# Values and gate of the retention layer: four pairs of k-tiles in seven products instead of three, in five of eight groups

## The chip, the core and the metric

The kernel runs on one core of a Trainium2 chip. The metric is the device time of one execution in microseconds (us). TensorE (PE) multiplies, VectorE (DVE) and ScalarE (ACT) do elementwise work, GpSimd (POOL) takes a few roots, SyncE (SP) issues the loads. Each engine runs its own list of instructions in the order written down when the program was built; an instruction that waits holds up everything behind it on its engine.

## The reference

A two-layer decoder trunk on 256 tokens of width 2048 in float32. Layer 0 mixes tokens by retention, layer 1 by latent attention, and a SwiGLU network follows each. The change lies in one product of the retention layer:

```python
def retention(x, positions, w_in, gn_g, w_out):
    proj = x @ w_in                       # 256 x 2048 by 2048 x 12288
    q, k, v, g = jnp.split(proj, [RET_QK, 2 * RET_QK, 2 * RET_QK + RET_VD], axis=-1)
    ...                                   # 8 heads; v and g have 512 columns per head
    scores = jnp.einsum('bhqd,bhkd->bhqk', qi, ki) * decay_in
    y = jnp.einsum('bhqk,bhkv->bhqv', scores, vi) + ...
    ...                                   # y is normalized per head
    out = (jax.nn.silu(g) * y)
    return out @ w_out
```

## The kernel before

**A float32 product in three.** Every operand is split into a rounded part (hi, a cast on ACT) and the rest (lo, a subtraction on DVE); `split` issues both. A product is then hi·hi + hi·lo + lo·hi: three matmuls of 128x512. The weights come from memory in tiles of 128 rows by 1024 columns (512 KB) and are split on the way, so a plain tile costs one ACT cast and one DVE subtraction of 128x1024.

**Groups.** Values and gate are made in eight groups `vg_group(0)` to `vg_group(7)`, one per head, names `rvg0` to `rvg7`. A group multiplies all 256 tokens (two halves of 128) by 1024 weight columns: 512 of v, 512 of the gate. It sums over 16 k-tiles in four PSUM banks `(t, c)`, t the token half and c the column half. A plain k-tile takes 12 matmuls.

**Seven products.** Two neighbouring k-tiles form a pair, and token half, column half and k-tile make it a 2x2 by 2x2 block product. `first_sevens` computes its first `n` pairs with seven block products instead of eight (Winograd's form of Strassen's scheme): 21 matmuls for 24. The sums of weight blocks are made on DVE, for every pair of every group. The left sums, of the input, are made once and kept in `ins[p]`. In words, for each pair `p`: `begin` loads two raw tiles `s0` and `s1`, makes t1, t2, t3 and splits b00, t2 (tile "b", two halves of 512) and t1, t3 (tile "a", 1024); `rest` splits the raw second tile (tile "c", 1024); `fourth` adds once more and splits the result (tile "d", 512).

```python
            b, a = parts("b"), parts("a")
            nc.vector.tensor_add(out=ta[:, 0:512], in0=b00, in1=b01)      # L458
            nc.vector.tensor_add(out=t2[p], in0=ta[:, 0:512], in1=b11)    # L459
            split(*half(b, 0), b00)
            split(*half(b, 1), t2[p])
            nc.vector.tensor_add(out=ta[:, 512:1024], in0=b01, in1=b11)   # L462
            split(*a, ta)
            ...
            split(*wt["c", p], raw1[p])                                   # rest
            ...
            nc.vector.tensor_add(out=t2[p], in0=t2[p], in1=raw1[p][:, 0:512])  # L473, fourth
            split(*wt["d", p], t2[p])
```

A group of values and gate therefore runs in four stretches on PE: A, the products of `begin` for all pairs (with the nine matmuls `ry` of the head before, of `mixed`, behind the first pair); B, those of `rest`, with DVE's sums `u`, `v` and c01, c11 over the banks (L485 to L495); C, those of `fourth`; D, the plain tiles, called by their k-tile `w6` to `w15`. Eight transposes `ztp` of the head before fall somewhere between. The feed-forward layers build their groups (`gu`) by the same function with four pairs, `GU_SEVENS = 4`.

**What orders the work.** The loads are all on SP's queue, the code is written in program order, and a scheduler then fixes each engine's list. Buffers are rings: 5 pairs of hi and lo tiles (`whi`, `wlo`, `WB`), 4 raw tiles (`raw`), 4 of tag `y4` for `s1`, 2 of `tsum` for `ta`. A new tile waits until the last reader of the one before it in its buffer is done. In the retention stage there are also 8 buffers of tag `yT`, one for each head's output; those not yet needed are lent to the last weight tiles of a group by `share(slots, room)`: `both` is 2 from six free slots, 1 from three, else 0 (hi and lo of so many last tiles), and `min(2, slots - 2 * both)` raw tiles (k-tiles 12 and 13; names with `x`). `later(k, fn)` runs a function k loading steps on.

Of the kernel before, what the change touches and what calls it, by code (L numbers as in the profile page):

```python
# [8 lines left out]
F32 = mybir.dt.float32  # L9
F32R = mybir.dt.float32r  # L10
# [5 lines left out]
P = 128  # L16
SEQ = 256
D = 2048
DT = D // P
NT = SEQ // P  # L20
EPS = 1e-6
RH, RK, RV = 8, 256, 512
# [13 lines left out]
DN_SEVENS = (2, 5, 7, 10, 12, 15, 17), (2, 4, 5, 7, 10, 12, 15, 17)  # L36
RTO_SEVENS = (3, 6, 9, 12), (3, 5, 6, 9, 12)
MLO_SEVENS = (3, 5), (1, 3)
QK_SEVENS, VG_SEVENS = (0, 2, 3, 3), 3

C_INV, C_ID, C_MASK, C_TWICE = 0, NF, NF + P, NF + 3 * P
C_DEC = C_TWICE + ROPE
# [16 lines left out]
def trunk(  # L59
# [19 lines left out]
    nc = tc.nc  # L79
# [8 lines left out]
    def misc_bank(name):  # L88
        return ps.tile([P, 512], F32, tag="misc", bufs=2, name=name)
# [43 lines left out]
    def later(k, fn):  # L133
        order[0] += 1
        todo.append((steps[0] + k, order[0], fn))
# [63 lines left out]
    wp = ctx.enter_context(tc.tile_pool(name="wp", bufs=1))  # L199
    RAW, WB, MV = 4, 5, 6  # L200

    def share(slots, room):

        both = 2 if slots >= 6 else 1 if slots >= 3 else 0
        return min(2, slots - 2 * both), both, room

    def split(hi, lo, src, g=None):

        if g is None:
            nc.scalar.copy(out=hi, in_=src)  # L210
            nc.vector.tensor_sub(out=lo, in0=src, in1=hi.bitcast(F32))  # L211
        else:
            nc.scalar.activation(out=hi, in_=src, func=AF.Copy, scale=g)
            nc.vector.scalar_tensor_tensor(
                out=lo, in0=src, scalar=g, in1=hi.bitcast(F32), op0=ALU.mult, op1=ALU.subtract
            )
# [18 lines left out]
    def gain(col, kt):  # L235
        return None if col is None else gcol[:, col + kt : col + kt + 1]
# [7 lines left out]
    def left_sums(a00, a01, a10, a11, sums, hi, lo):  # L244

        nc.vector.tensor_sub(out=sums[:, 0], in0=a10, in1=a11)
        nc.vector.tensor_sub(out=sums[:, 1], in0=sums[:, 0], in1=a00)
        nc.vector.tensor_sub(out=sums[:, 2], in0=a00, in1=a10)
        nc.vector.tensor_add(out=sums[:, 3], in0=sums[:, 1], in1=a01)
        split(hi, lo, sums)  # L250
# [321 lines left out]
    def hx(k):  # L572
        if k // 4 not in hT:
            hT[k // 4] = hp.tile([P, 4, 2, NT, P], F32R, tag="h8", bufs=4, name="hT")
        return hT[k // 4]
# [5 lines left out]
    def watched(pairs):  # L581


        made, held, tiles = {}, {}, [None]

        def seen(t, k0, n, part):
            for p in range(pairs):
                if k0 <= 2 * p < k0 + n:
                    held[t, p] = part[:, 2 * p - k0], part[:, 2 * p - k0 + 1]
                    if (1 - t, p) in held:  # L590
                        f, hi, lo = tiles[0](len(made))
                        left_sums(*held[0, p], *held[1, p], f, hi, lo)
                        made[p] = hi, lo

        watch[0] = seen
        return made, tiles
# [20 lines left out]
    def rms(ssq, n, tag, name):  # L617
        s = small(1, "s1", 4, f"{name}_s")
        nc.vector.tensor_reduce(out=s, in_=ssq, axis=mybir.AxisListType.X, op=ALU.add)
        v = small(1, "v1", 4, f"{name}_v")  # L620
        nc.vector.tensor_scalar(v, s, scalar1=1.0 / n, scalar2=EPS, op0=ALU.mult, op1=ALU.add)
        return rsqrt(v, 1, tag, 4, f"{name}_r")
# [141 lines left out]
    def retention():  # L764
# [15 lines left out]
            lo = wp.tile([P, 4, P], F32R, tag="al", bufs=3, name="rxl")  # L780
            return f, hi, lo

        ins, where = watched(max(*QK_SEVENS, VG_SEVENS))
        where[0] = tiles
        load_x(0, 0)
        later(0, lambda: norm_piece(0, 0, first[0], G_MIX))
# [12 lines left out]
        def qk_group(gq, spare):  # L799
            name = f"rqk{gq}"  # L800
            if gq:
                return first_sevens(h_lhs, DT, ret_qk, gq, name, QK_SEVENS[gq], lambda p: ins[p], spare)
            return group(h_lhs, DT, tile_load(ret_qk, gq, name, 1, spare), name, lead=3)

        def vg_group(h, spare):
            return first_sevens(h_lhs, DT, ret_vg, h, f"rvg{h}", VG_SEVENS, lambda p: ins[p], spare)

        with tc.tile_pool(name="rt_s", bufs=1) as sp:
            scores = {}
# [68 lines left out]
            with tc.tile_pool(name="rt_q", bufs=1) as rp, ExitStack() as copies:  # L878
                rope_c = rp.tile([P, NT, NF_R], F32, name="rope_c")
                rope_s = rp.tile([P, NT, NF_R], F32, name="rope_s")  # L880
                spare = share(3, lambda kind, name: rp.tile([P, 1024], kind, tag="spare", bufs=3, name=name))
                for gq in range(4):
                    banks = qk_group(gq, spare)
                    if gq == 0:
                        rx = [rms(first[t], D, "rx", f"first_r{t}") for t in range(NT)]
# [9 lines left out]
                banks = vg_group(0, spare)  # L895

            with tc.tile_pool(name="rt_v", bufs=1) as rp:

                yT = {}

                def spare_y(kind, name):
                    return rp.tile([P, 1024], kind, tag="yT", bufs=RH, name=name)

                def take_y(k0, n):
                    return yT[k0 // 4][:, k0 % 4 : k0 % 4 + n]

                def mixed(h, t, pr, v, sg):
                    y = misc_bank(f"ry{h}{t}")

                    terms = [  # L910
                        (pr[a][:, (kb + t) * P : (kb + t + 1) * P], v[b][:, kb, :])
                        for kb in range(t + 1)
                        for a, b in ((0, 0), (0, 1), (1, 0))
                    ]
                    for n, (left, right) in enumerate(terms):
                        nc.tensor.matmul(y, left, right, start=n == 0, stop=n == len(terms) - 1)  # L916
                    st = rp.tile([P, 6], F32, tag="bst", bufs=4, name="bst")
                    nc.vector.bn_stats(out=st, in_=y)
                    mv = rp.tile([P, 2], F32, tag="bmv", bufs=4, name="bmv")
                    nc.vector.bn_aggr(out=mv, in_=st)  # L920
                    ve = rp.tile([P, 1], F32, tag="bve", bufs=4, name="bve")
                    nc.vector.tensor_scalar(ve, mv[:, 1:2], scalar1=EPS, scalar2=None, op0=ALU.add)
                    rs = rsqrt(ve, 1, "grs", 4, "grs")
                    z = rp.tile([P, RV], F32, tag="z", bufs=2, name="z")
                    nc.vector.scalar_tensor_tensor(
                        out=z, in0=y, scalar=mv[:, 0:1], in1=sg[:, t, :],
                        op0=ALU.subtract, op1=ALU.mult,
                    )
                    nc.vector.tensor_scalar(z, z, scalar1=rs, scalar2=None, op0=ALU.mult)

                    def transposes():
                        if t == 0:
                            yT[h] = rp.tile([P, 4, NT, P], F32, tag="yT", bufs=RH, name=f"yT{h}")
                        tp = misc_bank(f"ztp{h}{t}")
                        for j in range(4):
                            nc.tensor.transpose(
                                tp[:, j * P : (j + 1) * P], z[:, j * P : (j + 1) * P], ident
                            )
                        for j in range(4):
                            nc.scalar.activation(  # L940
                                out=yT[h][:, j, t, :], in_=tp[:, j * P : (j + 1) * P], func=AF.Copy,
                                scale=gain(G_GN, h * 4 + j),
                            )

                    later(10, transposes)

                for h in range(RH):
                    if h:
                        banks = vg_group(h, share(RH - h, spare_y))
                    vh = rp.tile([P, NT, RV], F32R, tag="vh", bufs=1, name=f"vh{h}")  # L950
                    vl = rp.tile([P, NT, RV], F32R, tag="vl", bufs=1, name=f"vl{h}")
                    ph = rp.tile([P, 3 * P], F32R, tag="ph", bufs=1, name=f"ph{h}")
                    pl = rp.tile([P, 3 * P], F32R, tag="pl", bufs=1, name=f"pl{h}")
                    split(ph, pl, scores[h])
                    sg = rp.tile([P, NT, RV], F32, tag="sg", bufs=1, name=f"sg{h}")
                    for t in range(NT):
                        split(vh[:, t, :], vl[:, t, :], banks[t][0], rx[t])
                        nc.scalar.activation(
                            out=sg[:, t, :], in_=banks[t][1], func=AF.Silu, scale=rx[t]
                        )  # L960
                    for t in range(NT):
                        later(2 + t, lambda h=h, t=t, pr=(ph, pl), v=(vh, vl), sg=sg: mixed(h, t, pr, v, sg))

                gu_next[0] = watched(GU_SEVENS)
                closing(
                    take_y, RH * 4, ret_out, g_mix_post[0], G_FFN, "rto",
                    lambda name: rp.tile([P, 1024], F32, tag="sg", bufs=1, name=name), sevens=RTO_SEVENS,
                )
# [434 lines left out]
```

## Time and profile before

| | us |
|---|---|
| median of 3 runs | 2402.5 (2402.4 to 2402.98) |
| profiled execution | 2400.07 |
| its span, first to last instruction | 2398.3 |
| busy in the span: PE / DVE / ACT / POOL | 2382.3 / 2179.7 / 1500.3 / 28.5 |
| granted PE clock | 0.999 |
| stage of the eight groups of values and gate | about 197 to 556 |
| one such group, from one head's `ry` to the next | 44.7 |
| one `gu` group of the first feed-forward layer | 41.7 |

Times inside the profile count from the start of the span. "Busy" of PE covers overlapping matmuls, so how fast PE goes is read from the distance between the starts of matmuls or of stretches, not from their durations. The chain in the page is followed back from the last instruction.

### The profile page before, as it was taken

What the parts mean: (1) busy time and instruction counts of PE and PEld (TensorE: products, weight loads), DVE (VectorE), ACT (ScalarE), POOL (GpSimd) and SP (SyncE); (2) the same over time, 40 slices, a digit from 0 to 9 for tenths busy, and PEclk for the clock granted to TensorE, in tenths of its full rate; (3) what the DMA queues carried; (4) which work ended last, traced back from release to release, by engine and by line L of the source; (5) the groups of instructions that cost most, each with busy time, mean ns of one, the idle gap of its engine ahead of it and who ended that gap; (6) DMA issues with size and microseconds to landing.
All of it is one profiled execution on the core that took longest, in us unless ns stands there. A gap on an engine that the chain in (4) does not pass through costs nothing.

```text
span 2398.3 us, 30805 instructions
## 1 busy us (share of the span) xinstructions
PE 2382.3 (99%) x10843; PEld 1971.0 (82%) x10843; DVE 2179.7 (91%) x3112; ACT 1500.3 (63%) x2126; POOL 28.5 (1%) x38
## 2 busy tenths in 40 slices
PE   9999999999999999999999999999999999999998
PEld 7888888888888888888888888887888888888887
DVE  8899888888899999999988987889999999998998
ACT  6555665665666656666666666656666665666664
POOL 0000000000000000000000000000100000000000
PEclk9999999999999999999999999999999999999999
DMA  8555465545656665656456655445666565645655
GB/s 285 187 195 191 167 212 184 170 170 192 206 194 219 207 207 199 209 179 219 161 197 210 200 196 158 129 138 171 234 205 216 177 218 184 212 167 183 221 199 168
DMA packets 129611, 463.76 MB, mean 193 GB/s; under 512 B 14640, under 2 KB 15024, under 8 KB 129456
## 3 DMA queue, kind: packets, MB, share of 16 engines
q1 hardware_dynamic: 129456, 461.80, 57.7%
q8 instruction: 85, 1.39, 0.2%
q14 instruction: 70, 0.57, 0.1%
HBM read 459.64 MB, written 2.10 MB: 193 GB/s over the span
## 4 chain that ended last, share of the span: by engine, by line
PE 94%; DVE 4%; DMA 1%; issue 1%; ACT 1%; SPq 0%; POOL 0%; DVEq 0%; POOLq 0%; ACTq 0%
PE gu_b L419 37%; PE dn_b L419 15%; PE rvg_b L419 14%; PE rqk_b L419 6%; PE rto_b L419 6%; PE q L419 3%; PE dn_m L419 3%; PE mlo_b L419 2%; PE mc_b L419 1%; PE rto_m L419 1%; PE ftp L988 1%; PE ry L916 1%; PE htp L602 0%; PE rsc L861 0%; PE asc L1240 0%
## 5 line engine op out<-in xcount | busy, mean ns | idle before, releaser
L419 PE MATMUL gu_b<-gu_w_hi,hT 128*128 128x512 f32 x1296 | 353.6, 391 | 0.1
L419 PEld LDWEIGHTS gu_b<-gu_w_hi,hT 128*128 128x128 f32 x1296 | 242.3, 188 | 50.6 <-DVE hT L211 0.9
L210 ACT CAST dn_w_hi<-dn_w_raw 128x1024 fp32r<-128x1024 f32 (+1 forms) x176 | 169.1, 978 | 78.4 <-DMA dn_w_raw<-w_down 33.7
L419 PE MATMUL gu_b<-gu_w_lo,hT 128*128 128x512 f32 x648 | 200.4, 391 | 0.0
L211 DVE TENSOR_TENSOR dn_w_lo<-dn_w_raw,dn_w_hi 128x1024 fp32r<-128x1024 f32 (+1 forms) x176 | 193.8, 1130 | 7.1 <-ACT dn_w_hi L210 6.3
L419 PE MATMUL rvg_b<-rvg_w_hi,hT 128*128 128x512 f32 x576 | 157.4, 391 | 0.0
L419 PE MATMUL dn_b<-dn_w_lo,dn_ah 128*128 128x512 f32 x494 | 156.7, 390 | 0.3 <-DVE dn_w_lo L211 0.3
L419 PE MATMUL dn_b<-dn_w_hi,dn_ah 128*128 128x512 f32 x494 | 156.7, 390 | 0.0
L419 PE MATMUL dn_b<-dn_w_hi,dn_al 128*128 128x512 f32 x494 | 156.7, 390 | 0.0
L211 DVE TENSOR_TENSOR gu_w_lo<-gu_w_raw,gu_w_hi 128x1024 fp32r<-128x1024 f32 x122 | 143.6, 1223 | 6.0 <-ACT gu_w_hi L210 6.0
L419 PEld LDWEIGHTS gu_b<-gu_w_lo,hT 128*128 128x128 f32 x648 | 121.2, 188 | 26.3 <-DVE gu_w_lo L211 1.5
L210 ACT CAST gu_w_hi<-gu_w_raw 128x1024 fp32r<-128x1024 f32 x122 | 122.5, 1049 | 29.2 <-PE gu_b L419 11.3
L419 PEld LDWEIGHTS rvg_b<-rvg_w_hi,hT 128*128 128x128 f32 x576 | 107.7, 188 | 22.0
L210 ACT CAST gu_ahi<-gu_ta 128x1024 fp32r<-128x1024 f32 x80 | 84.4, 1055 | 46.7 <-PE gu_b L419 36.0
L211 DVE TENSOR_TENSOR gu_clo<-gu_s,gu_chi 128x1024 fp32r<-128x1024 f32 x80 | 97.6, 1222 | 14.7 <-ACT gu_chi L210 13.4
L419 PEld LDWEIGHTS dn_b<-dn_w_lo,dn_ah 128*128 128x128 f32 x494 | 92.7, 188 | 19.8 <-DVE dn_w_lo L211 0.7
L419 PEld LDWEIGHTS dn_b<-dn_w_hi,dn_ah 128*128 128x128 f32 x494 | 92.8, 188 | 19.2
L419 PEld LDWEIGHTS dn_b<-dn_w_hi,dn_al 128*128 128x128 f32 x494 | 92.8, 188 | 19.2
L211 DVE TENSOR_TENSOR gu_alo<-gu_ta,gu_ahi 128x1024 fp32r<-128x1024 f32 x80 | 97.8, 1223 | 7.0 <-ACT gu_ahi L210 6.9
L210 ACT CAST gu_bhi<-gu_s 128x512 fp32r<-128x512 f32 x80 | 49.7, 622 | 81.6 <-PE gu_b L419 65.9
L419 PE MATMUL rqk_b<-rqk_w_hi,hT 128*128 128x512 f32 x352 | 99.4, 396 | 1.2 <-ACT rqk_w_hi L210 1.1
L210 ACT CAST gu_chi<-gu_s 128x1024 fp32r<-128x1024 f32 x80 | 83.8, 1051 | 13.6 <-PE gu_b L419 13.4
(535 smaller groups left out, 6284.9 us busy)
## 6 DMA issues: line engine op xcount, KB each, us to landing
dn_w_raw<-w_down SPq DMA_DIRECT2D x176, 512.0 KB, 4.5
gu_s<-w_gu SPq DMA_DIRECT2D x160, 512.0 KB, 4.6
gu_w_raw<-w_gu SPq DMA_DIRECT2D x152, 512.0 KB, 3.7
rvg_w_raw<-ret_vg SPq DMA_DIRECT2D x67, 512.0 KB, 4.4
rto_w_raw<-ret_out SPq DMA_DIRECT2D x64, 512.0 KB, 4.3
rvg_s<-ret_vg SPq DMA_DIRECT2D x48, 512.0 KB, 4.2
rqk_w_raw<-ret_qk SPq DMA_DIRECT2D x43, 512.0 KB, 4.3
gu_w_xraw<-w_gu SPq DMA_DIRECT2D x40, 512.0 KB, 5.2
```

The source lines that it names most:

```text
L210: nc.scalar.copy(out=hi, in_=src)
L211: nc.vector.tensor_sub(out=lo, in0=src, in1=hi.bitcast(F32))
L419: nc.tensor.matmul(out, e[2](), e[3](), start=bank not in begun, stop=ends[bank, added.get(bank, 0)] == n, skip_group_check=bank in added,)
L916: nc.tensor.matmul(y, left, right, start=n == 0, stop=n == len(terms) - 1)
L988: nc.tensor.transpose(tp[:, b * P : (b + 1) * P], a[:, b * P : (b + 1) * P], ident)
```

## The change

Groups 2 to 6 of values and gate take four pairs by seven products; groups 0, 1 and 7 stay at three. The left sums of the fourth pair (k-tiles 6 and 7) are made by a new function `fourth_sums`, which a `later(9, ...)` puts into group 1: it adds the hi and lo parts of both k-tiles of the input together again, makes the four sums, splits them and keeps both parts in one `yT` buffer. That buffer is missing from the slots that groups 2 to 6 may lend out, so `share` gets one less there: group 2 lends one hi and lo pair instead of two, group 4 one raw tile instead of two, group 5 no hi and lo pair and two raw tiles instead of one each, group 6 one raw tile instead of two; group 3 lends as before.

```diff
-QK_SEVENS, VG_SEVENS = (0, 2, 3, 3), 3
+QK_SEVENS, VG_SEVENS = (0, 2, 3, 3), (3, 3, 4, 4, 4, 4, 4, 3)
...
-        ins, where = watched(max(*QK_SEVENS, VG_SEVENS))
+        ins, where = watched(3)
...
-            return first_sevens(h_lhs, DT, ret_vg, h, f"rvg{h}", VG_SEVENS, lambda p: ins[p], spare)
+            return first_sevens(h_lhs, DT, ret_vg, h, f"rvg{h}", VG_SEVENS[h], lambda p: ins[p], spare)
...
+                def fourth_sums():
+
+                    a, f = (
+                        wp.tile([P, 512], F32, tag="mv", bufs=MV, name=f"rx{n}").rearrange(
+                            "p (j q) -> p j q", j=4
+                        )
+                        for n in ("a", "f")
+                    )
+                    h = hx(6)[:, 2:4].bitcast(F32)
+                    nc.vector.tensor_add(
+                        out=a.rearrange("p (k t) q -> p k t q", k=2), in0=h[:, :, 0], in1=h[:, :, 1]
+                    )
+                    both = spare_y(F32R, "rxs").rearrange("p (n j q) -> p n j q", n=2, j=4)
+                    left_sums(a[:, 0], a[:, 2], a[:, 1], a[:, 3], f, both[:, 0], both[:, 1])
+                    ins[3] = both[:, 0], both[:, 1]
+
+                later(9, fourth_sums)
...
-                        banks = vg_group(h, share(RH - h, spare_y))
+                        banks = vg_group(h, share(RH - h - (2 <= h < 7), spare_y))
```

The lists of the engines change in order, too. On DVE, the place at the end of stretch A in group 5, from the split of the last pair's "a" tile to that of the first "c" tile (`bst`, `bmv`, `bve`, `z` are the normalization of head 4, `pl5` the split of the scores of head 5). Before:

```order
L211 TENSOR_TENSOR rvg5_alo_3965<-rvg5_ta_3960,rvg5_ahi_3964 128x1024
L918 BN_STATS bst_3896<-ry40_3892 128x6
L918 BN_STATS bst_3916<-ry41_3909 128x6
L920 BN_AGGR bmv_3898<-bst_3896 128x2
L211 TENSOR_TENSOR pl5_4252<-pr21_1782,ph5_4251 128x384
L922 TENSOR_SCALAR bve_3900<-bmv_3898 128x1
L925 SCALAR_TENSOR_TENSOR z_3904<-ry40_3892,bmv_3898,sg4_3853 128x512
L920 BN_AGGR bmv_3918<-bst_3916 128x2
L929 TENSOR_SCALAR z_3904<-z_3904,grs_3902 128x512
L922 TENSOR_SCALAR bve_3920<-bmv_3918 128x1
L925 SCALAR_TENSOR_TENSOR z_3924<-ry41_3909,bmv_3918,sg4_3853 128x512
L211 TENSOR_TENSOR rvg5_clo_3999<-rvg5_s1_3866,rvg5_chi_3998 128x1024
```

The same place after the change:

```order
L211 TENSOR_TENSOR rvg5_blo_4037<-rvg5_s0_4030,rvg5_bhi_4036 128x512
L947 TENSOR_SCALAR z_3967<-z_3967,grs_3965 128x512
L211 TENSOR_TENSOR rvg5_blo_4037<-rvg5_t2_4035,rvg5_bhi_4036 128x512
L462 TENSOR_TENSOR rvg5_ta_4034<-rvg5_s0_4030,rvg5_s1_4032 128x512
L473 TENSOR_TENSOR rvg5_t2_3912<-rvg5_t2_3912,rvg5_s1_3909 128x512
L473 TENSOR_TENSOR rvg5_t2_3973<-rvg5_t2_3973,rvg5_s1_3970 128x512
L485 TENSOR_TENSOR rvg5_mv1_4057<-rvg5_b01_3904,rvg5_mv0_4052 128x512
L211 TENSOR_TENSOR rvg5_alo_4039<-rvg5_ta_4034,rvg5_ahi_4038 128x1024
L211 TENSOR_TENSOR rvg5_clo_4073<-rvg5_s1_3909,rvg5_chi_4072 128x1024
```

The normalization of the head before now comes ahead of the last pair's "a" tile instead of behind it, and the adds of `fourth` (L473), which stood in the group before and in stretch A's start, are behind it.

On DVE, the end of stretch B and stretch C in group 3. Before:

```order
L211 TENSOR_TENSOR rvg3_clo_3209<-rvg3_s1_3154,rvg3_chi_3208 128x1024
L495 TENSOR_TENSOR rvg3_b11_3059<-rvg3_b11_3059,rvg3_mv0_3174 128x512
L211 TENSOR_TENSOR rvg3_dlo_3225<-rvg3_t2_3065,rvg3_dhi_3224 128x512
L211 TENSOR_TENSOR rvg3_dlo_3225<-rvg3_t2_3126,rvg3_dhi_3224 128x512
L211 TENSOR_TENSOR rvg3_dlo_3239<-rvg3_t2_3157,rvg3_dhi_3238 128x512
L211 TENSOR_TENSOR rvg3_w6_lo_3249<-rvg3_w6_raw_3246,rvg3_w6_hi_3248 128x1024
```

After:

```order
L211 TENSOR_TENSOR rvg3_clo_3268<-rvg3_s1_3206,rvg3_chi_3267 128x1024
L473 TENSOR_TENSOR rvg3_t2_3086<-rvg3_t2_3086,rvg3_s1_3083 128x512
L473 TENSOR_TENSOR rvg3_t2_3147<-rvg3_t2_3147,rvg3_s1_3144 128x512
L473 TENSOR_TENSOR rvg3_t2_3178<-rvg3_t2_3178,rvg3_s1_3175 128x512
L211 TENSOR_TENSOR rvg3_dlo_3287<-rvg3_t2_3086,rvg3_dhi_3286 128x512
L211 TENSOR_TENSOR rvg3_dlo_3287<-rvg3_t2_3147,rvg3_dhi_3286 128x512
L211 TENSOR_TENSOR rvg3_dlo_3301<-rvg3_t2_3178,rvg3_dhi_3300 128x512
L473 TENSOR_TENSOR rvg3_t2_3209<-rvg3_t2_3209,rvg3_s1_3206 128x512
L211 TENSOR_TENSOR rvg3_w8_lo_3317<-rvg3_w8_raw_3314,rvg3_w8_hi_3316 128x1024
L211 TENSOR_TENSOR rvg3_dlo_3301<-rvg3_t2_3209,rvg3_dhi_3300 128x512
```

Four adds of `fourth` that stood in the stretches before now stand between the last "c" tile and the "d" tiles, and the last "d" tile has gone behind the first plain tile.

## The prediction

> **What bounds the kernel now.** I read the page's busy times first, then the chain that ended last for its shares by engine.
>
> ```profile
> PE 2382.3 (99%) x10843; PEld 1971.0 (82%) x10843; DVE 2179.7 (91%) x3112; ACT 1500.3 (63%) x2126; POOL 28.5 (1%) x38
> PE 94%; DVE 4%; DMA 1%; issue 1%; ACT 1%; SPq 0%; POOL 0%; DVEq 0%; POOLq 0%; ACTq 0%
> ```
>
> PE sets the end and DVE is close behind. So a change that takes matmuls away and gives DVE work has to be read in its own stage. Next the chain inside that stage (start, length, what; x counts instructions), two rounds of it:
>
> ```profile
> 424.24 2.04 PE ry L916 x9
> 426.28 7.73 PE rvg_b L419 x34
> ...
> 460.92 0.44 PE ztp L936 x4
> 461.36 7.59 PE rvg_b L419 x33
> 468.95 2.04 PE ry L916 x9
> ```
>
> Nothing but PE stands in it: one group of values and gate takes 468.95 - 424.24 = 44.71 us, and a matmul of 128x512 takes 7.73 / 34 = 0.227 us of PE's time. Then the busy times of whole groups by engine (columns: length, PE, PEld, DVE, ACT, POOL, clock, DMA share, GB/s): one group of this stage, then three of the first feed-forward layer, which run four pairs already.
>
> ```profile
> 379.51:424.23 44.72, 44.72 (x202) 36.79 (x201) 39.29 (x54) 27.61 (x41) 1.09 (x2) 1.00 0.55 177
> 1031.88:1073.62 41.74, 41.74 (x190) 34.63 (x189) 39.72 (x52) 26.59 (x34) 0.00 (x0) 1.00 0.59 202
> 1073.61:1115.35 41.74, 41.74 (x190) 34.62 (x189) 38.87 (x51) 26.48 (x34) 0.00 (x0) 1.00 0.61 202
> 1115.35:1157.09 41.74, 41.74 (x191) 34.64 (x189) 38.44 (x49) 26.05 (x34) 0.00 (x0) 1.00 0.60 201
> ```
>
> DVE has 44.72 - 39.29 = 5.4 us idle in a values-and-gate group. In the feed-forward groups it has 2.0 to 3.3 us idle, and PE still keeps an even 41.74. That 2.0 is the least DVE idle seen in a group that PE runs through.
>
> **The change, part by part.**
>
> *PE.* A pair in seven products takes 21 matmuls for 24. Five groups save 15: 15 x 0.227 = 3.4 us, all on the chain. A group would then last 44.72 - 0.68 = 44.04. The duration column is no price here: these matmuls show about 390 ns each and would give 5.9 us, but they start 0.227 apart.
>
> *DVE, amount.* For one more pair `begin` has three adds and `fourth` one (512 wide). The lo parts of b, t2 and d are three more of 512, and those of a and c are two of 1024, which replace the two of the plain tiles. The price is the distance of starts:
>
> ```profile
> 363.59 0.68 DVE L462 TENSOR_TENSOR rvg_ta<-rvg_s,rvg_s 128x512 f32<-128x512 f32 x1
> 364.20 0.68 DVE L211 TENSOR_TENSOR rvg_blo<-rvg_s,rvg_bhi 128x512 fp32r<-128x512 f32 x1
> 364.80 0.68 DVE L211 TENSOR_TENSOR rvg_blo<-rvg_t,rvg_bhi 128x512 fp32r<-128x512 f32 x1
> ```
>
> Starts are 0.60 apart, so seven more cost 4.2 us a group. DVE then needs 39.29 + 4.2 = 43.5 of 44.04 us: 0.5 us, or 1%, is left for all its waits. From 87.9% it goes to 98.8%.
>
> The Trainium skill speaks against such a change: "VectorE: DVE Perf Modes", section "The DRAIN you can't avoid", says that an operation does not start until the pipe of the one before has emptied, and the section "Rules for kernel authors" therefore asks for few operations. Here starts are 0.60 us apart at a duration of 0.68, so successive operations overlap and the measurement decides. By a strict reading of that rule the seven would cost 7 x 0.68 = 4.8 us a group, and the result would be five times 0.6 = 3 us worse than mine.
>
> *DVE, waits.* Which of its idle remains? First what it waits for today in the group 379.51 to 424.23 (total, times, longest), then in the three feed-forward groups in turn: 1031.88 to 1073.62 (two raw tiles lent, as in groups 2 and 3 now), 1073.61 to 1115.35 (one lent, as in group 4; the rows that repeat are left out) and, of the third (two lent and no hi and lo pair, as in group 5), the row that is new:
>
> ```profile
> DVE rvg_w_lo L211 <- ACT rvg_w_hi L210: 2.6, 3, 2.0
> DVE rvg_blo L211 <- ACT rvg_bhi L210: 1.5, 1, 1.5
> DVE rvg_alo L211 <- ACT rvg_ahi L210: 1.3, 1, 1.3
> ```
>
> ```profile
> DVE gu_clo L211 <- ACT gu_chi L210: 0.7, 1, 0.7
> DVE gu_w_xlo L211 <- ACT gu_w_xhi L210: 0.4, 1, 0.4
> DVE gu_blo L211 <- ACT gu_bhi L210: 0.4, 1, 0.4
> DVE gu_w_lo L211 <- ACT gu_w_hi L210: 0.3, 1, 0.3
> ```
>
> ```profile
> DVE gu_w_lo L211 <- ACT gu_w_hi L210: 1.8, 2, 1.3
> ```
>
> ```profile
> DVE gu_ta L458 <- DMA gu_s<-w_gu: 1.5, 1, 1.5
> ```
>
> The waits for b, a and c are of an engine that is early: the cast before them waits until PE frees one of the five hi and lo buffers. They shrink as DVE gets later. The waits for plain tiles (w, xlo) stay: raw tile 12 can be loaded only when tile 8's subtraction is done, and its cast waits for that load.
>
> ```profile
> 349.41 3.73 SPq L555 DMA_DIRECT2D rvg_w_raw<-ret_vg  x4
> 354.12 1.05 ACT L210 CAST rvg_w_hi<-rvg_w_raw 128x1024 fp32r<-128x1024 f32 x1 [3.93 <-DMA rvg_w_raw<-ret_vg]
> rvg_w_raw<-ret_vg SPq DMA_DIRECT2D x67, 512.0 KB, 4.4
> ```
>
> So 0.7 us stays where two raw tiles are lent (groups 2, 3, 5) and 1.8 us where one is (4, 6). What goes beyond the 0.5 us left is PE's: 3 x 0.2 + 2 x 1.3 = 3.2 us. The ends of this unknown: zero, if order and buffers hide these waits too, and 5 x (2.0 - 0.5) = 7.5 us, if the least idle seen stays whole; five times the 3.3 of the last feed-forward group would be 14. I take 3.2, nearer to zero, because DVE comes later to every load than in these rows. For that reason I also count the 1.5 us of the third group, a wait for the raw tile that comes after the plain ones, as gone; if it stays, group 5 adds 1.5.
>
> *The places of use* say the same. The tightest group for comparison, 1110 to 1131: its first product, the last "a" tile made and used, the third and fourth "c", the "d" tiles made, the fourth "c" used, the first "d" used.
>
> ```profile
> 1110.43 0.39 PE L419 MATMUL gu_b<-gu_bhi,hT 128*128 128x512 f32 x1
> 1117.05 1.22 DVE L211 TENSOR_TENSOR gu_alo<-gu_ta,gu_ahi 128x1024 fp32r<-128x1024 f32 x1
> 1120.39 0.39 PE L419 MATMUL gu_b<-gu_alo,sh 128*128 128x512 f32 x1
> 1124.16 1.22 DVE L211 TENSOR_TENSOR gu_clo<-gu_s,gu_chi 128x1024 fp32r<-128x1024 f32 x1
> 1125.89 2.49 DVE L211 TENSOR_TENSOR gu_dlo<-gu_t,gu_dhi 128x512 fp32r<-128x512 f32 x4
> 1125.62 0.40 PE L419 MATMUL gu_b<-gu_clo,hT 128*128 128x512 f32 x1
> 1127.89 0.39 PE L419 MATMUL gu_b<-gu_dlo,hT 128*128 128x512 f32 x1
> ```
>
> The margins are 1120.39 - 1118.27 = 2.1 us at the last "a", 0.2 at the fourth "c", 1.3 at the first "d". Values and gate add the normalization and `pl` in stretch A:
>
> ```profile
> 336.39 1.29 DVE L918 BATCH_NORM_STATS2 bst<-ry 128x6 f32<-128x512 f32 x2
> 340.17 1.21 DVE L211 TENSOR_TENSOR rvg_clo<-rvg_s,rvg_chi 128x1024 fp32r<-128x1024 f32 x1
> ```
>
> That is 3.8 us of DVE against 2.04 us of PE's `ry`: 1.7 less margin. Hence 0.4 is left at "a" and -0.4 at "d", before the adds of `fourth` that the list of group 3 puts ahead of the "d" tiles (three, 1.8 us). Behind a late "d" stand the plain tiles on DVE and the same bank's matmuls on PE, so a wait there is paid in full.
>
> *The fourth left sums.* One add of 512, four of 128 wide, one cast, one lo part in group 1. By the rows 0.60 + 4 x 0.29 + 0.60 = 2.4 us, covered by idle time in group 1:
>
> ```profile
> L247 DVE TENSOR_TENSOR dn_sf<-dn_sf,aT x16: 284/288/303, 1180.2 to 2267.0; 128x128 f32<-128x128 f32 x16
> 244.39:289.11 44.72, 44.72 (x200) 36.71 (x201) 40.62 (x56) 28.82 (x43) 1.10 (x2) 1.00 0.60 201
> ```
>
> 4.1 us are idle there; without that cover it costs up to 2.4. I take 0.
>
> *Loads, ACT, POOL.* The number of loads stays at 16 of 512 KB a group. All four `y4` buffers are now in use, so the first `s1` of the next group no longer comes a group ahead and stands on SP's queue with the others, ahead of the raw tiles. At 177 to 202 GB/s and a DMA share under 0.61 I charge nothing beyond the waits above. ACT gets three casts of 512, 1.9 us on 27.6 of 44.7. POOL's list is unchanged.
>
> *Sum.* -3.4 + 3.2 = -0.2 us. The profiled execution took 2400.07 (span 2398.3), which would become 2399.9. It is 2.4 below the median of the runs, 2402.5; carried over, the median becomes 2402.3.
>
> **The rivals.**
>
> *All waits hidden.* PE keeps its pace: -3.4, so 2399.1. For it: in the feed-forward stage PE shows no wait down to 2.0 us of DVE idle. Against it: only 0.5 is left here.
>
> *DVE takes over as the bound.* Each group lasts as long as DVE's 43.5 us plus its idle. With the 2.0 us seen, 45.5: +0.8 a group, +4.0 in all, 2406.5. With the 3.3 of the last feed-forward group 46.8, so +10, 2412.5. For it: the "d" tiles with negative margin, and the longer waits where one raw tile is lent. It decides from 1.2 us of remaining idle on (no gain); from 2.2 us on the whole is slower by 0.2%. Against it: the scheduler's lists use DVE's early waits for work that came later.
>
> *The seven products don't pay at all on PE*, because the missing matmuls were not all on the chain: the chain of the stage is only PE, so hardly.
>
> **How the numbers follow.** About 0.2%, 4.8 us, is what a measurement of this kernel can tell from no change. My forecast, between -2.4 and +2.5, has 0.46; all hidden, -4.4 to -2.4, 0.28; DVE as the bound 0.22, of which 0.04 below +4.8; faster than -4.8 would need more than the whole saving and gets 0.04. Within 0.2%: 0.46 + 0.28 + 0.04 = 0.78; slower 0.18; faster 0.04. The range reaches from all hidden with half a microsecond for the measurement, 2398.6, to +5, 2407.5; it leaves out the upper part of DVE's case and little below.
>
> **What would show it.** Right: groups 2 to 6 last between 44.0 and 45.2, DVE about 43.5 busy in each, PE waiting at L419 for `rvg_dlo`, `rvg_alo` or `rvg_clo`, most after groups 4 and 6; group 1 as long as before. Wrong: groups of 44.04 with no such waits (all hidden), or 45.5 and more; a DVE busy time off 43.5; a change outside 197 to 556 us.

## The result: 0.3% slower, and most of it in one group

The changed kernel takes 2408.36 us (median of 11 runs) against 2402.92 of the kernel before (11 runs on the same chip); the ratio is 1.003, with a 95% interval of 1.0021 to 1.0038 (both are taken over all the runs; the two medians alone are 5.4 us, or 0.23%, apart). That is slower, and outside the range of the prediction by 0.9 us. The profiled execution took 2407.39, its span is 2405.6. The first page of the profile, and the chain that ended last:

```profile
PE 2384.1 (99%) x10828; PEld 1966.6 (82%) x10828; DVE 2201.0 (91%) x3153; ACT 1507.1 (63%) x2142; POOL 28.5 (1%) x38
PE 89%; DVE 7%; DMA 1%; issue 1%; ACT 1%; SPq 0%; POOL 0%; DVEq 0%; POOLq 0%; ACTq 0%
```

The chain now names a load of this stage, `rvg_w_xraw`, with 1%. A look at the stage group by group is clearer. The view by stretches, cut at the first `ry` matmul of each group, for groups 1 to 7 (length, busy time of PE, PEld, DVE, ACT and POOL with instructions, granted PE clock, DMA share, GB/s):

```profile
243.29:288.92 45.63, 45.63 (x205) 37.38 (x204) 42.63 (x62) 30.32 (x45) 1.10 (x2) 1.00 0.57 198
288.92:341.75 52.83, 48.09 (x198) 38.09 (x197) 42.37 (x61) 28.63 (x44) 1.10 (x2) 0.94 0.47 159
341.75:386.26 44.51, 44.48 (x198) 36.20 (x197) 43.66 (x63) 29.29 (x44) 1.10 (x2) 1.00 0.51 177
386.26:430.56 44.30, 44.30 (x198) 36.29 (x197) 40.83 (x58) 28.40 (x43) 1.10 (x2) 1.00 0.56 190
430.56:477.22 46.66, 45.67 (x198) 35.92 (x197) 45.25 (x65) 28.32 (x43) 1.10 (x2) 1.00 0.50 169
477.22:522.21 44.99, 44.76 (x199) 35.99 (x197) 42.59 (x61) 28.52 (x44) 1.10 (x2) 1.00 0.53 176
522.21:570.06 47.85, 47.85 (x216) 39.64 (x215) 43.41 (x70) 32.33 (x47) 1.09 (x2) 1.00 0.50 170
```

Before, groups 2 to 6 lasted 44.7 each; group 2 then:

```profile
289.86:334.61 44.75, 44.75 (x202) 36.83 (x200) 39.29 (x54) 27.60 (x41) 1.09 (x2) 1.00 0.56 188
```

At PE's pace with four pairs they should last 44.04 (44.72 less 0.68). Above that are 8.8 us in group 2, 0.5 in group 3, 0.3 in group 4, 2.6 in group 5 and 0.9 in group 6. Groups 1 and 7 are as before. Groups 1 to 7 together went from 317.0 to 326.8. What lies outside groups 1 to 7 is nearly the same code in all kernels of this study, and took between 2078.8 and 2083.0 us in its fifteen profiles at full clock (span less the sum of the groups). The changed kernel's profile has the least of these, and the one before 2081.3; so the two spans differ by 7.3 us where the stage differs by 9.7. A pair of profiles therefore tells the stage's loss, and the runs the whole's.

**What happens in group 2.** The timeline of the changed kernel, at the end of the group (start, duration, engine, line, out<-in; in brackets the idle time before it and its releaser):

```profile
322.99 0.82 PE L954 MATMUL ztp<-cst,z 128*128 128x128 f32 x6
323.41 2.17 ACT L958 ACTIVATE yT<-ztp,gcol 128x128 f32<-128x128 f32 x8 [11.86 <-PE ztp L954]
325.42 1.09 ACT L210 CAST rvg_w_xhi<-rvg_w_raw 128x1024 fp32r<-128x1024 f32 x1
326.35 1.10 ACT L210 CAST rvg_w_hi<-rvg_w_xraw 128x1024 fp32r<-128x1024 f32 x1
326.55 1.22 DVE L211 TENSOR_TENSOR rvg_w_xlo<-rvg_w_raw,rvg_w_xhi 128x1024 fp32r<-128x1024 f32 x1 [5.42 <-ACT rvg_w_xhi L210]
327.51 0.73 PE L419 MATMUL rvg_b<-rvg_w_hi,hT 128*128 128x512 f32 x2 [3.70 <-ACT rvg_w_hi L210]
328.96 1.22 PE L419 MATMUL rvg_b<-rvg_w_lo,hT 128*128 128x512 f32 x2 [0.72 <-DVE rvg_w_lo L211]
335.06 1.09 PE L419 MATMUL rvg_b<-rvg_w_hi,hT 128*128 128x512 f32 x4
```

ACT stands still for 11.86 us. It is at the eight copies `yT` of the head before, and these wait for transposes `ztp`, which stand on PE behind k-tile 12. Behind the copies on ACT stand the casts of k-tiles 15, 13 and 14. So PE works up to its transposes, frees ACT, and then has to wait itself until ACT has done eight copies (2.2 us) and two casts: it stands still for 3.70 us and once more for 0.72. Below, these eight copies ahead of casts that PE needs next are called the block. ACT's list from k-tile 12 to the first cast of group 3, in the changed kernel and, below, before (without the numbers at the rows' starts):

```
L210 CAST rvg2_w12_hi_2975<-rvg2_w12_xraw_2973 128x1024
L958 ACTIVATE yT1_2991<-ztp10_2992,gcol_74 128x128 x4
L958 ACTIVATE yT1_2991<-ztp11_3019,gcol_74 128x128 x4
L210 CAST rvg2_w15_xhi_3048<-rvg2_w15_raw_3046 128x1024
L210 CAST rvg2_w13_hi_3003<-rvg2_w13_xraw_3001 128x1024
L210 CAST rvg2_w14_hi_3030<-rvg2_w14_raw_3028 128x1024
L210 CAST rvg3_bhi_3087<-rvg3_s0_3081 128x512
```

```
L210 CAST rvg2_w12_hi_2954<-rvg2_w12_xraw_2952 128x1024
L210 CAST rvg2_w14_xhi_3009<-rvg2_w14_raw_3007 128x1024
L210 CAST rvg2_w13_hi_2982<-rvg2_w13_xraw_2980 128x1024
L210 CAST rvg2_w15_xhi_3027<-rvg2_w15_raw_3025 128x1024
L210 CAST rvg3_bhi_3066<-rvg3_s0_3060 128x512
```

Before, four of the eight copies came right after the `d` tiles, and the other four among the next group's first casts; they waited 0.23 us and nothing:

```profile
300.28 1.14 ACT L940 ACTIVATE yT<-ztp,gcol 128x128 f32<-128x128 f32 x4 [0.23 <-PE ztp L936]
327.28 1.13 ACT L940 ACTIVATE yT<-ztp,gcol 128x128 f32<-128x128 f32 x4
```

**A stop costs more than its length.** The same view by stretches, for the stop and what follows it:

```profile
322.99:327.51 4.52, 0.82 (x7) 0.58 (x5) 0.96 (x1) 4.10 (x11) 0.00 (x0) 1.00 0.00 0
327.51:331.00 3.49, 2.77 (x7) 1.95 (x8) 3.49 (x5) 3.49 (x6) 0.00 (x0) 0.59 0.42 150
331.00:335.00 4.00, 4.00 (x11) 3.13 (x10) 2.88 (x5) 1.47 (x2) 0.00 (x0) 0.50 0.94 321
335.00:341.75 6.75, 6.75 (x30) 5.45 (x30) 6.19 (x10) 3.98 (x7) 0.00 (x0) 1.00 0.35 123
```

After the stop the granted clock is 0.59 and 0.50 on average in these stretches; in finer ones it is 1.00 up to 328.2, 0.50 from there to 335.0, and 1.00 again. From 327.51 to 335.06 PE gets through 16 matmuls; less the wait of 0.72 that is 6.8 us, where 16 x 0.227 = 3.6 would do. So the 8.8 us of group 2 are 4.4 of standing still, 3.2 of half clock, and 1.2 that are left, small waits earlier in the group for the most part. The Trainium skill, "TensorE: Matmul & The Clock Gate", section "Part 1: The HAM clock gate (the "warmup" mystery)", says that PE falls to half its clock after an idle window of about 3.4 us and comes back after it has been busy for about as long. The trace agrees on the stop (3.70) and on the half (0.50); coming back took 6.8 us here, with another wait in between.

### The profile page after: what moved, and what is told of

It is laid out like the page before. It is cut to its first block, busy times and chain, and to the rows that moved or that the text cites. A ratio compares the mean times of both kernels' runs of the same rounds, so it can differ in the third digit from the quotient of the medians.

```text
span 2405.6 us, 30831 instructions
## 1 busy us (share of the span) xinstructions
PE 2384.1 (99%) x10828; PEld 1966.6 (82%) x10828; DVE 2201.0 (91%) x3153; ACT 1507.1 (63%) x2142; POOL 28.5 (1%) x38
## 4 chain that ended last, share of the span: by engine, by line
PE 89%; DVE 7%; DMA 1%; issue 1%; ACT 1%; SPq 0%; POOL 0%; DVEq 0%; POOLq 0%; ACTq 0%
PE gu_b L419 38%; PE dn_b L419 14%; PE rvg_b L419 9%; PE rto_b L419 6%; PE rqk_b L419 6%; PE dn_m L419 3%; PE q L419 3%; PE mlo_b L419 2%; PE mc_b L419 1%; PE rto_m L419 1%; PE ftp L1006 1%; DMA rvg_w_xraw<-ret_vg 1%; PE asc L1258 0%; PE rsc L861 0%; PE asc L1255 0%
## 5 line engine op out<-in xcount | busy, mean ns | idle before, releaser
L419 PE MATMUL rvg_b<-rvg_w_hi,hT 128*128 128x512 f32 x512 | 142.2, 394 | 4.2 <-ACT rvg_w_hi L210 4.2
L419 PEld LDWEIGHTS rvg_b<-rvg_w_hi,hT 128*128 128x128 f32 x512 | 97.1, 190 | 25.0 <-ACT rvg_w_hi L210 4.7
```

Of the source, the lines that this page charges most:

```text
L419: nc.tensor.matmul(out, e[2](), e[3](), start=bank not in begun, stop=ends[bank, added.get(bank, 0)] == n, skip_group_check=bank in added,)
```

## The experiments

The theories, in short: (1) the scheduler's list for ACT in group 2 is an accident, and blocks; what DVE loses besides comes out as PE's waiting, since it has so little to spare; (2) four pairs keep DVE too busy in any order; (3) the `yT` buffer that is no longer lent is the cause. Group lengths of all profiles, in us (read as above; the sum is of groups 1 to 7; runs e1 to e14 are in the order of the text):

| | g2 | g3 | g4 | g5 | g6 | sum 1-7 | median, ratio to before |
|---|---|---|---|---|---|---|---|
| before | 44.75 | 44.74 | 44.72 | 44.72 | 44.67 | 317.0 | |
| changed | 52.83 | 44.51 | 44.30 | 46.66 | 44.99 | 326.8 | 1.0030 (1.0021-1.0038) |
| e1 | 44.76 | 44.23 | 48.09 | 44.41 | 45.01 | 320.0 | 1.0000 (0.9991-1.0009) |
| e2 | 44.68 | 51.42 | 45.52 | 45.73 | 45.64 | 326.5 | one run, 2410.07 |
| e4 | 44.68 | 44.73 | 44.67 | 44.69 | 44.47 | 316.7 | one run, 2400.3 |
| e5 | 44.48 | 44.13 | 44.87 | 45.82 | 45.01 | 318.1 | 1.0000 (0.9991-1.0009) |
| e6 | 44.51 | 44.13 | 44.77 | 45.24 | 45.04 | 317.2 | one run, 2398.22 |
| e7 | 44.11 | 44.24 | 46.33 | 44.66 | 44.22 | 317.1 | 0.9991 (0.9982-1.0000) |
| e8 | 44.52 | 44.05 | 44.37 | 44.42 | 44.21 | 315.2 | one run, 2400.09 |
| e9 | 44.75 | 44.22 | 46.01 | 44.53 | 45.03 | 318.3 | 0.9998 (0.9989-1.0007) |
| e10 | 44.14 | 44.80 | 45.28 | 46.24 | 44.98 | 318.9 | one run, 2400.01 |
| e11 | 44.04 | 44.04 | 43.94 | 45.32 | 45.35 | 316.2 | 0.9992 (0.9983-1.0001) |
| e12 | 44.40 | 44.50 | 44.95 | 46.12 | 46.09 | 319.6 | 1.0008 (1.0000-1.0017) |
| e13 | 44.16 | 44.03 | 43.91 | 44.60 | 44.84 | 315.0 | 0.9988 (0.9979-0.9997) |
| e14 | 44.04 | 44.03 | 44.03 | 44.83 | 44.28 | 314.7 | 0.9984 (0.9975-0.9993) |

### e1: transposes due earlier

```diff
-                    later(10, transposes)
+                    later(6, transposes)
```

> The changed kernel, but the transposes of each head (ztp) and their copies (yT) are due 6 loading steps on instead of 10; in ACT's list they then stand between casts whose tiles come later, never as a block of eight ahead of the last tiles' casts in group 2. Theory 1 (an accident of ACT's list: in group 2 eight copies wait for transposes behind k-tile 12 on PE, and the casts of k-tiles 13 to 15 wait behind the copies): group 2 falls from 52.8 to 44.0-45.0 us, the other groups stay within 1 us, the whole gains 7 to 9 us on the changed kernel and ends at about 0.1% faster than before (ratio 0.997 to 1.000). Theory 2 (four pairs keep DVE or the buffers too busy in group 2, whatever the order): group 2 stays above 50, ratio to before 1.003. Theory 3 (only the missing lent buffers): as theory 2.

Group 2 is back at 44.76 with all four pairs and the same lent buffers: theories 2 and 3 fall for group 2. The whole came out at 2403.0 (before 2402.22), as fast as before and no more, because group 4 lasts 48.1. The row of group 3's waits and the stretches of groups 3 and 4:

```profile
ACT yT L958 <- PE ztp L954: 3.3, 1, 3.3
334.59:378.82 44.23, 44.23 (x199) 36.17 (x197) 38.43 (x55) 27.57 (x42) 1.10 (x2) 1.00 0.51 179
378.82:426.91 48.09, 46.03 (x198) 35.77 (x197) 46.69 (x68) 30.43 (x46) 1.10 (x2) 1.00 0.55 186
```

In group 3 a smaller block stands on ACT, late in the group. PE isn't hurt at once; but DVE does only 38.4 us of work there and has 46.7 to do in the next group, more than PE needs for that group. A delay on DVE seems to be paid one group later; the windows show it so, and no run tests it by itself.

### e2: three pairs in group 2

```diff
-..., VG_SEVENS = ..., (3, 3, 4, 4, 4, 4, 4, 3)
+..., VG_SEVENS = ..., (3, 3, 3, 4, 4, 4, 4, 3)
```

> The changed kernel with three pairs in group 2 and four in groups 3 to 6; buffers are lent as in the changed kernel. In ACT's list the block of eight copies ahead of the last casts now stands in group 3 (after the cast of k-tile 12), with the transposes behind k-tile 12 on PE. Theory 1 (the list): group 2 is back at 44.7 us, group 3 takes over the loss and lasts 50 to 54 instead of 44.5, the whole is within 2 us of the changed kernel. Theory 2 or 3 (something in group 2 itself: its loads, its lent buffers, four pairs after a group with three): group 2 at 44.7, group 3 at 44 to 46, the whole 7 to 8 us shorter than the changed kernel.

The loss moves to group 3, 51.42 us, as theory 1 said from the list. The timeline shows the same picture there:

```profile
368.45 2.17 ACT L958 ACTIVATE yT<-ztp,gcol 128x128 f32<-128x128 f32 x8 [10.61 <-PE ztp L954]
372.55 1.22 PE L419 MATMUL rvg_b<-rvg_w_hi,hT 128*128 128x512 f32 x2 [3.70 <-ACT rvg_w_hi L210]
372.50:379.50 7.00, 6.72 (x16) 4.88 (x17) 6.13 (x8) 4.79 (x7) 0.00 (x0) 0.55 0.68 240
```

The half clock after the stop comes again as well, 0.55 over 7 us.

### e3 and e10: fewer buffers lent in group 2

```diff
+ (0, 1, spare_y) if h == 2 else share(RH - h - (2 <= h < 7), spare_y)   # raw tiles, pairs: the function
+                                                                         # returns raw tiles first
```

Group 2 lends no raw tile and one hi and lo pair here: two raw tiles fewer than in the changed kernel (in both expectations the two kinds of buffer are mixed up).

> The changed kernel, but group 2 lends only one raw tile (k-tile 13) and no hi and lo pair, instead of two raw tiles and one pair: four buffers fewer. In ACT's list the eight copies of group 2 then stand behind the casts of k-tiles 13 and 14, in group 3. Theory 1 (the list): group 2 falls from 52.8 to 44.0-46.0 us although it has fewer buffers; 7 to 9 us less in all. Theory 3 (the buffers lent are too few): group 2 gets longer still, above 53.

That run had a granted clock of 0.654 from its first to its last microsecond and took 3418.71 us; it tells nothing of the groups. The same kernel ran again as e10, on another chip.

> The kernel of the third experiment once more, since that run had a granted clock of 0.654 throughout and tells nothing of the groups at full clock: group 2 lends one raw tile and no hi and lo pair, and in ACT's list its eight copies stand behind the casts of k-tiles 13 and 14. Theory 1 (the list): group 2 at 44.0-46.0 although it has three buffers fewer. Theory 3 (the lent buffers): above 53.

Group 2 lasts 44.14, the pace of PE, with two buffers fewer. In this list the casts of k-tiles 13 and 14 stand ahead of the copies, which come among the next group's first casts. Theory 3 is out for group 2: it isn't the buffers that are missing, it is the order.

### e4: three pairs everywhere, the rest of the change kept

```diff
-..., VG_SEVENS = ..., (3, 3, 4, 4, 4, 4, 4, 3)
+..., VG_SEVENS = ..., (3, 3, 3, 3, 3, 3, 3, 3)
```

> The changed kernel with three pairs in all groups: what stays of the change is the making of the fourth left sums in group 1 (not used) and the buffer that is missing from those lent in groups 2 to 6. All theories: PE is the bound with three pairs. Theory 1: groups 2 to 6 last 44.7 each as before, total within 1 us of before. Theory 3 (the missing buffers cost by themselves): groups 4 and 6, with one lent raw tile instead of two, or group 2, with one lent pair instead of two, longer by 1 us or more.

All groups are as before (44.5 to 44.7), group 1 with the left sums at 45.62. The sums of the input and the missing buffer cost nothing by themselves.

### e5: transposes due 5 steps on, and e9: those of one head alone

```diff
-                    later(10, transposes)
+                    later(5, transposes)                      # e5
+                    later(5 if h == 1 else 10, transposes)    # e9
```

> The changed kernel with the transposes due 5 loading steps on (10 in the changed kernel, 6 in the first experiment). On PE they now stand ahead of k-tile 9 in every group from 2 to 6, so the copies on ACT wait for nothing, wherever they stand among the casts. In the first experiment group 2 was back at 44.8 us, but in group 3 eight copies ahead of the cast of k-tile 12 still held ACT up 3.3 us, and group 4 lasted 48.1. Theory 1 (blocks in ACT's list, and DVE with so little to spare that what it loses in one group comes out as PE's waiting in the next): groups 2 to 6 at 44.0-45.0 each, groups 1 to 7 together 315 to 318 us (317.0 before, 326.8 changed), ratio to before 0.997-0.999. Theory 2 (DVE is the bound of four pairs by itself): groups at 45 and more, together 320 or more, ratio 1.000 or above.

> The changed kernel with the transposes of head 1 alone due 5 loading steps on; all other heads at 10 as in the changed kernel. Of the lists, what matters changes in group 2: its transposes stand ahead of k-tile 9 on PE. Theory 1: group 2 at 44.0-45.0 instead of 52.8, the other groups within 1 us of the changed kernel unless another block of copies forms (in group 3 eight copies now stand ahead of the casts of k-tiles 13 to 15, but their transposes come early on PE, so they should wait for nothing): 7 to 8.5 us less than the changed kernel, ratio to before 0.999-1.001. Theory 2: group 2 above 50.

By their ratios both take some 7 us off the changed kernel, and end where the kernel before stands: 2401.79 against 2401.28, and 2401.31 against 2401.01. In e9 one head's transposes are all that was changed in the code, and group 2 falls by 8.1 us; its group 4 is 1.7 longer than in the changed kernel, where the scheduler's lists for groups 3 and 4 come out otherwise too. Eight copies still stand ahead of the last casts there, and ACT waits for them, but their transposes stand ahead of k-tile 9 on PE, which has work meanwhile:

```profile
312.96 1.15 ACT L958 ACTIVATE yT<-ztp,gcol 128x128 f32<-128x128 f32 x4 [2.49 <-PE ztp L954]
313.97 2.01 ACT L210 CAST rvg_w_hi<-rvg_w_xraw 128x1024 fp32r<-128x1024 f32 x2
```

What is left above 44.04 in groups 2 to 6 is 4.1 us in e5 and 4.3 in e9, more than the 3.4 that PE saves. e5 was expected at 0.997 to 0.999 and came out at 1.0000: the block is the slowdown, but without it the change is only even.

### e6: two raw tiles and no pair lent in group 4

```diff
+ (2, 0, spare_y) if h == 4 else share(RH - h - (2 <= h < 7), spare_y)   # on e5
```

> As the run with 5 steps, but group 4 lends two raw tiles and no hi and lo pair, instead of one and one. If the late load of k-tile 13 in group 4 (one raw tile lent) is what makes group 5 long (46.7 us in the changed kernel), group 5 lasts 44.0-44.6 here and is shorter than in the run with 5 steps by what that one has above 44.1. If group 5 is long for another reason (its own lent tiles, DVE's own work), it is as long as in the run with 5 steps, within 0.2 us.

Group 4 gets a second raw tile here and gives up its hi and lo pair for it. Group 5 falls from 45.82 to 45.24, not to 44.6: this exchange is worth a third of what group 5 loses. What the raw tile alone is worth isn't shown, since the pair went with it.

### e7 and e8: the scaling taken off DVE

```diff
-                    nc.vector.tensor_scalar(z, z, scalar1=rs, scalar2=None, op0=ALU.mult)
+                    nc.scalar.activation(out=z, in_=z, func=AF.Copy, scale=rs)   # e7, on e5; e8: neither
```

> As the run with 5 steps, but the last scaling of the normalized output (z times grs, two instructions of 128x512 a group) runs on ACT instead of DVE: 1.2 us a group less on DVE, and as much more on ACT. Theory 1: what is left of PE's waiting goes, as DVE then has 1.7 us a group to spare instead of 0.5: groups 2 to 6 at 44.0-44.3, groups 1 to 7 together 314 to 316 us, ratio to before 0.996-0.998. Theory 2 (DVE's work alone): the groups get shorter by up to 1.2 us each. Rival: the scaling waits on ACT for DVE and POOL and holds the casts up: groups 45 and more.

> As the run with 5 steps, with that scaling left out altogether in all heads (so the output lacks it): DVE 1.2 us a group less, nothing more on ACT. Theory 1: groups 2 to 6 at 44.0-44.3; where they are longer, a wait for a load or a block in ACT's list must show. Theory 2: as the run with 5 steps less up to 1.2 us a group.

e8 leaves the scaling out, so its output lacks it. Two scalings were put at 1.2 us; in e5 the next row on DVE starts 0.40 us after one, so they are 0.8 a group:

```profile
297.09 0.48 DVE L947 TENSOR_SCALAR z<-z,grs 128x512 f32<-128x512 f32 x1
297.49 0.14 DVE L940 TENSOR_SCALAR bve<-bmv 128x1 f32<-128x1 f32 x1
```

DVE's busy time in groups 2 to 6 falls by as much, from 43.0 a group on average (e5) to 42.2 (e7 and e8). In e8 these groups lose 1.4 us in all where e5 loses 4.1. That points to DVE's lack of reserve as the larger part of what e5 had left; but the lists come out otherwise too, and e8 is a single profile. Three groups of e8 are at 44.4 to 44.5, just above what theory 1 gave. With the scaling on ACT (e7) the five groups lose 3.4, more than theory 1 allowed, and the ratio misses its 0.996 to 0.998: four groups behave as in e8, and group 4 doesn't (46.33). Its rows name `rvg_blo`, `rvg_dlo` and casts that wait for raw tiles, and its list differs from its neighbours'; which of these began it wasn't settled.

### e11 and e12: an even list

e11 is e7 with the transposes due 4 steps on and two raw tiles and no pair lent in group 4; e12 has 3 steps.

> Scaling on ACT as in the seventh experiment, transposes due 4 steps on, and group 4 lends two raw tiles. In all groups from 2 to 6 the second head half's transposes now stand ahead of k-tile 8 on PE, and no cast stands behind a copy that waits. Theory 1: groups 2 to 6 at 44.0-44.4, together with groups 1 and 7 314 to 315.5 us, ratio to before 0.9980-0.9995. If group 4 or 5 stays at 45 and more, the loads of the last k-tiles are the rest.

> As the run before, with the transposes due 3 steps on: all eight stand in stretch A on PE. Theory 1: as the run before, if the scaled output is ready by then (about 9.5 us into the group); if not, PE waits for it, and groups are longer than in the run before by that wait, up to 2 us each.

In e11 groups 2, 3 and 4 run at 44.04, 44.04 and 43.94: PE's pace, the whole saving of 0.7 each. Groups 5 and 6 stay at 45.3, which theory 1 as it stood doesn't give. In e12 PE doesn't wait for the scaled output, as I had thought it might. The rows of group 2 show another block on ACT: the eight copies now stand ahead of the copy of the first bank (L481), from which DVE makes its sums (L485), for which PE waits (L492):

```profile
DVE rvg_mv L485 <- ACT rvg_mv L481: 0.8, 1, 0.8
PEld rvg_b L419 <- DVE rvg_b L492: 0.5, 1, 0.5
```

### e13 and e14: groups 5 and 6

```diff
+ VG_SEVENS (3, 3, 4, 4, 4, 3, 3, 3); share as before the change for groups 5 and 6            # e13, on e11
+ (0, 1, spare_y) if h == 5 else share(RH - h - (2 <= h < 7), spare_y)                         # e14, on e11
```

> As the run with the scaling on ACT and 4 steps, but four pairs in groups 2, 3 and 4 only; groups 5 and 6 are back at three pairs and lend what they did before the change. Theory 1: groups 2 to 4 at 44.0-44.1, groups 5 and 6 at 44.7 or a little less, groups 1 to 7 together 314.8-315.4 us (317.0 before, 316.2 in the run it comes from), so 1.7 to 2.2 us faster than before by the stage, ratio 0.9988-0.9995. If group 5, which follows a group without a lent pair, is at 45.5 and more, the missing pair costs three pairs as well.

> As the run with the scaling on ACT and 4 steps, but group 4 lends one raw tile and one hi and lo pair (two raw tiles there), and group 5 one pair (two raw tiles there). If the missing pair made the first tiles of groups 5 and 6 late (the rows show the last tiles of the group before in the ring of five), groups 5 and 6 fall from 45.3 to 44.0-44.5. If the raw tiles matter more, or DVE's own work, they stay at 45.3 or get longer, and group 4's and 5's last tiles wait for loads.

In e14 group 4 lends one raw tile and one pair again (in e11 two raw tiles), and group 5 one pair in place of its two raw tiles. Group 6 falls from 45.35 to 44.28 and group 5 from 45.32 to 44.83: 1.6 of the 2.6 us that they had above PE's pace. The rows of e11's group 5, PE's wait and the two of ACT ahead of it, and below them group 5's wait for a load and the stretch of group 6 in e14:

```profile
PE rvg_b L419 <- DVE rvg_clo L211: 0.6, 1, 0.6
ACT rvg_w_hi L210 <- PE rvg_b L419: 5.3, 4, 1.7
ACT rvg_bhi L210 <- PE rvg_b L419: 4.4, 3, 1.7
```

```profile
ACT rvg_w_hi L210 <- DMA rvg_w_raw<-ret_vg: 3.5, 3, 2.7
466.26:510.54 44.28, 44.22 (x199) 36.22 (x197) 42.38 (x60) 29.31 (x45) 1.10 (x2) 1.00 0.50 168
```

A reading of these rows: where no pair is lent, all last tiles take places in the ring of five, ACT waits for PE to free them, and the next group's tiles are made late, up to the `c` tiles. With three pairs (e13) the same late start costs nothing, 44.60.

That the missing pair is the cause isn't shown. In e7 groups 4 and 5 lend what they lend in the changed kernel, group 5 no pair, and group 5's window has the same wait, yet group 6 lasts 44.22 (the row of the wait, the stretch of group 6):

```profile
ACT rvg_bhi L210 <- PE rvg_b L419: 4.4, 3, 1.7
469.07:513.29 44.22, 44.22 (x199) 36.12 (x197) 41.96 (x59) 29.91 (x46) 1.10 (x2) 1.00 0.52 179
```

And e6 made the exchange of e14's group 4 the other way, a raw tile for the pair, and group 5 got shorter there too, by 0.6. So the lists have a part in it that these runs don't separate from the buffers. In e14 group 5 keeps 0.8, beside a wait for raw tiles in place of the one for the ring. e14 beats both kernels: 2397.65 us against 2401.29 before, ratio 0.9984 with an interval of 0.9975 to 0.9993; e13 beats the kernel before as well, 0.9988 (0.9979 to 0.9997).

## Why the prediction was wrong, by its own steps

**PE's saving, -3.4: right.** Groups 2 to 4 of e11 and of e14 last 44.03 to 44.04 (one 43.94), 0.7 under the 44.7 of before.

**The fourth left sums, 0: right.** Group 1 took 45.63 against 45.58, and 45.62 in e4.

**PE's waits, 3.2: the step that failed is group 2's share of 0.2.** It came from DVE's waits for loads that would stay. Group 2's loss of 8.8 has nothing to do with those: it is ACT's list. The sentence at fault is "ACT gets three casts of 512, 1.9 us on 27.6 of 44.7", for which nothing was charged. It weighs an engine by its busy time, and ACT was busy 28.6 of 52.8 us in group 2, with 11.9 of standing at one copy. What counts on an engine with a fixed list is which row stands ahead of which, and for whom each one waits. The prediction looked at DVE's rows in groups 3 and 5; ACT's rows in group 2, and PE's `ztp` behind k-tile 12, stood in the changed kernel's lists and weren't read. That the whole ended only 0.9 us beyond the range is luck: 8.8 of the 13.1 us that groups 2 to 6 lost came from where 0.2 had been put down. The front part says that the eight transposes fall "somewhere between"; that is the place where it happened.

**The rest of the waits: about the right sum, in the wrong places.** Groups 3 to 6 lost 4.3 us where 3.0 was put down for them; without the block (e5) all five lost 4.1 for 3.2. The 1.3 us "after groups 4 and 6", for one lent raw tile, were to be seen in group 5 as 2.6 (1.8 in e5) and in group 6 as 0.9; a second raw tile in place of the pair in group 4 takes a third of the 1.8 away (e6). Which buffers are lent beyond the raw tiles was charged nothing, and the exchanges of e14 took 1.6 us off groups 5 and 6; why stays open.

**DVE as the bound: part of a rival.** The prediction gave it 0.22. It seems to decide after the block is gone: 0.8 us a group less on DVE and nothing more on ACT goes with 2.7 of the 4.1 us (e5, e8). With the scaling on ACT only 0.8 of them go (e7). DVE was busy 42.9 us a group on average instead of the 43.5 put down, and what it missed in one group it did in the next (40.8, then 45.3, in groups 4 and 5).

**The signs that were named.** PE's waits for `clo` and `alo` came, most of all in group 5 (its weight loads, in the view of waits):

```profile
PEld rvg_b L419 <- DVE rvg_clo L211: 0.9, 2, 0.5
PEld rvg_b L419 <- DVE rvg_alo L211: 0.6, 1, 0.6
```

They were small beside group 2's wait for a cast, which wasn't named. No change outside the stage was seen, beyond what any two profiles differ by.

**The prices.** Had the lists been those of e5, -0.2 would have been 0.9 off (4.1 - 3.4 = +0.7 us; e5's median stood 0.5 above that of before). The list turned it into +7.2 us by the ratio (5.0 to 9.1).

## What to carry to other kernels

When a change makes a scheduler write new lists, read every engine's list around the places where engines hand over to one another, the little used engines above all: a cheap row that waits for a late producer holds up every row behind it. An engine that just keeps up, as DVE did here, can pay for a delay one stage later, so give it some reserve before shortening the work of the one it feeds. Count a long stop of PE at more than its length: 4.4 us cost 7.6 here.

## What the hardware showed that was not expected

- After a stop of 3.70 us PE's granted clock was 0.50 for 6.8 us, in two kernels (changed, from 328.2 to 335.0 us; e2, from 371.9 to 378.7). Single waits of up to 1.5 us in the middle of the kernel (e1, at 1747) left the clock at 1.00; none between 1.5 and 3.7 us was seen there.
- A long single stop isn't the only thing that lowers the clock. In eight of the fifteen profiles at full clock it also fell to 0.50 once in the first 16 us, for 3.4 us (6.8 in e5), where no wait of PE was longer than 1.4 us. In the kernel before, from 9.35 to 12.76 us, PE had been busy for 1.86 of the 3.35 us ahead of that. What the condition is, is open.
- One execution (e3) had a granted clock of 0.654 throughout and took 3418.71 us; the same kernel took 2400.01 the next time, on another chip (e10). Other runs on the first chip in the same session were at 0.997 to 0.999. Why is open.
